# SBUF addresses of attention outputs and of the low part of x's transpose in a two-layer decoder trunk

## The chip, the cores and the metric

The kernel runs on one core of a Trainium2 chip. The metric is the device time of one execution in microseconds; several executions are timed and the median is given. One further execution was profiled.

## What is computed

Two decoder layers on 256 tokens of width 1024, float32 throughout. Cut to what matters:

```python
def hybrid_mixer(x, w_in, w_branch_sb, w_branch_moba, w_out):
    proj = x @ w_in                       # 1024 -> 3*512 + 3*512 + 2*1024
    q_sb, k_sb, v_sb, q_mb, k_mb, v_mb, g_sb, g_mb = jnp.split(proj, cuts, axis=-1)
    o_sb = stick_breaking_attention(heads(q_sb, 8), heads(k_sb, 8), heads(v_sb, 8))
    o_mb = moba_attention(partial_rope(...), partial_rope(...), heads(v_mb, 8))
    merged = jax.nn.sigmoid(g_sb) * (merge_heads(o_sb) @ w_branch_sb) \
           + jax.nn.sigmoid(g_mb) * (merge_heads(o_mb) @ w_branch_moba)
    return merged @ w_out

def swiglu(x, w_gate, w_up, w_down):      # 1024 -> 2816 -> 1024
    return (jax.nn.silu(x @ w_gate) * (x @ w_up)) @ w_down

for l in range(2):
    x = layer_norm(DEEPNORM_ALPHA * x + hybrid_mixer(x, ...), ln_mix_g[l], ln_mix_b[l])
    x = layer_norm(DEEPNORM_ALPHA * x + swiglu(x, ...), ln_ffn_g[l], ln_ffn_b[l])
```

## The kernel before, in words

Each float32 operand of a matmul is split into two parts, hi (rounded to the type float32r) and lo (the rest), and each product is three matmuls: hi by hi, and hi by lo both ways (`mm3`, line 281; every matmul is issued by `mm`, line 275). A matmul has a stationary operand, which a weight load (LDWEIGHTS, engine PEld) puts into the array, and a moving operand, which then streams through it. Every matmul has its own load, and the load of the next runs beside the matmul at work.

The weights stream in as 245 granules of 128 x 1024 from DRAM (`raw`), are cast by ACT (line 48) to `whi`, and subtracted by DVE (line 53) to `wlo`. Ten split granules and four raw ones have fixed places in SBUF. A small planner (`Weave`) decides while the program is built when the side lines (attention, norms, splits) are emitted between the main line of projections; each engine then works in that fixed order.

The stages of a layer, by the names of their PSUM tiles:

- `pvq`, `pk`, `pu`, `pft`: token-major products of x (`tok_major`, line 305). Stationary is a 128-token part of `xT_hi` or `xT_lo`, the weights stream, 512 columns.
- `pqk` (q and k of the sticks), `pg` (gates), `pf` (18 chunks of the gate and up products of SwiGLU): feature-major products of x (`feat_major`, line 327). Stationary are the weights, and `xT_hi` or `xT_lo` streams, 256 columns. The three come in the order (xT_hi, whi), (xT_lo, whi), (xT_hi, wlo).
- `sb_s`, `sb_o` and the like: the attention itself, its results written to `osb_hi/lo` (line 615) and `omb_hi/lo` (line 654).
- `pb`: the branch projections (lines 671 to 685). Stationary are the weights, the attention outputs stream, 256 columns.
- `pw`: the output projection, `pd` and (for the second half of the tokens in the last layer) `pe`: the down projection (`token_out`, line 336). Stationary is the merged branch m or the SwiGLU product h, the weights stream; `pe` in columns of 512, 256 and 256.

All long-lived activations (v, q, k, osb, omb, gates, m, h, layer norm parameters) are 4 KB tiles from one pool `acts` with 15 buffers (line 186), handed out in turn as they become free; x's transpose lies in two tiles of a pool `const` (lines 218 and 219). A tile's address in its partition follows from the pools in the order in which they are made and from the sizes in them. As the built programs place them, in bytes modulo 512:

| tile | before | after |
|---|---|---|
| xT_hi | 384 | 384 |
| xT_lo | 384 | 0 |
| whi, wlo, raw | 448 | 448 |
| osb, omb; h0 and h1 in the same buffers | 448 | 0 |
| v, q_mb, k_mb, gates, m, other h, ln | 448 | 448 |
| work tiles (q, k, attention weights) | 448 | 64 |

Each tile's slices (256 tokens, 128 tokens, 128 weight columns of 4 bytes) begin at multiples of 512 bytes from its start, so that all of them share the tile's place modulo 512.

Of the kernel before, what the change touches and what calls it, by code (L numbers as in the profile page):

```python
# [7 lines left out]
F32 = mybir.dt.float32  # L8
F32R = mybir.dt.float32r
# [5 lines left out]
P = 128  # L15
# [19 lines left out]
class Weave:  # L35
    """Program order: the main line of projections, with side lines (attention, norms,
    rotary, weight splits) woven in. Every engine takes its instructions in program order,
    so each is emitted about when its operands are there, by an estimate of the time at
    which each engine gets through what it has been given. A side line yields the time
    at which it goes on; on the tensor engine's clock."""  # L40

# [40 lines left out]
    def start(self, gen):  # L82
        """A side line whose first stage comes now."""
        side = self.add(gen)
        if not self.busy:
            self._step(side)
        return side
# [9 lines left out]
class WeightStream:  # L97
    """Weight granules [128, 1024]: loaded in float32, then split exactly into
    two float32r parts (hi = rounded, lo = the rest) for the tensor engine."""

# [24 lines left out]
    def line(self):  # L125
        """The side line: a granule at a time, as far as the buffers allow."""
        nc, weave = self.nc, self.weave
        while self.split < self.total:
            g = self.split
            ahead = g - self.current  # L130
            if g > self.limit:
                yield weave.t + 0.1
                continue
            if ahead >= LEAD and max(weave.dve_t, weave.act_t) > weave.t + BACKLOG:
                yield weave.t + 0.2
                continue
            self.load(g + NRAW)
            if ahead > 0:
                yield self.there[g]
            hi, lo = (self.pool.tile([P, GCOLS], F32R, tag=n, name=f"{n}{g}", bufs=NSPLIT)  # L140
                      for n in ("whi", "wlo"))
            t = self.raw.pop(g)
            n = GCOLS // len(self._pieces(g))
            for sl in self._pieces(g):
                e = weave.act(self.there[g], n, nc.scalar.copy, hi[:, sl], t[:, sl])
            if g - self.current > 0:
                yield e
            for sl in self._pieces(g):
                e = weave.dve(e, n, nc.vector.tensor_sub, lo[:, sl], t[:, sl], hi[:, sl].bitcast(F32))
            self.parts[g], self.ready[g] = (hi, lo), e  # L150
            self.split += 1
            self.load(g + 1 + NRAW)

    def allow(self, g):
        """Granule g's buffers are free from here on."""
        self.limit = max(self.limit, min(g, self.total - 1))
# [7 lines left out]


NRAW = 4
NSPLIT = 10
# [12 lines left out]
def hybrid_trunk_kernel(ctx: ExitStack, tc: tile.TileContext, w, xT_in, x_in, ln_in,  # L180
# [4 lines left out]
    wpool = ctx.enter_context(tc.tile_pool(name="wpool", bufs=1))  # L185
    acts = ctx.enter_context(tc.tile_pool(name="acts", bufs=15))
    work = ctx.enter_context(tc.tile_pool(name="work", bufs=3))
# [5 lines left out]

    def unit(name, shape, dt=F32):
        return acts.tile(shape, dt, tag="u4", name=name)

    def pair_tiles(name, shape):
        return unit(name + "_hi", shape, F32R), unit(name + "_lo", shape, F32R)

# [12 lines left out]

# [1 line left out]
    xT_raw = [unit(f"xT_raw{t}", [P, KC, P]) for t in range(2)]  # L214
    ident = const.tile([P, P], F32, name="ident")
    rope = const.tile([P, 2, 2, ROPE], F32, name="rope")
    xs = [const.tile([P, D], F32, name=f"x{t}") for t in range(2)]
    xT_hi = const.tile([P, KC, S], F32R, name="xT_hi")
    xT_lo = const.tile([P, KC, S], F32R, name="xT_lo")
    mask = const.tile([P, 2, P], F32, name="mask")  # L220
    zero = const.tile([P, 1], F32, name="zero")
# [5 lines left out]
    nc.scalar.activation(warm, zero, AF.Sigmoid)  # L227
    # The tensor engine's clock rises after some microseconds of work: give it zeros meanwhile.
    idle = unit("idle", [P, 512], F32R)
# [42 lines left out]

# [1 line left out]
    def mm(o, a, b, start, stop):  # L274
# [30 lines left out]
    def tok_major(o, g, t, first, last, k0):  # L305
        """o[tokens of t, 512] += x @ granule g ([2 kc, 512])."""
        hi, lo = ws.take(g)
        hi = hi.rearrange("p (k c) -> p k c", k=2)
        lo = lo.rearrange("p (k c) -> p k c", k=2)
        for k in range(2):  # L310
            ts = slice(t * P, (t + 1) * P)
            mm3(o, xT_hi[:, k0 + k, ts], xT_lo[:, k0 + k, ts], hi[:, k, :], lo[:, k, :],
                first and k == 0, last and k == 1)

    def both_tokens(name, g0, put):
        """All tokens of x @ granules g0..g0+3; put(tokens, bank) takes each half."""
        acc = [bankM(f"{name}{t}", [P, WIDTH]) for t in range(2)]
        order = ((0, 0), (1, 0), (0, 1), (1, 1), (0, 2), (0, 3)) if g0 == 0 else \
            ((0, 0), (0, 1), (0, 2), (1, 0), (1, 1), (0, 3))
        for t, k in order + ((1, 2), (1, 3)):  # L320
            tok_major(acc[t], g0 + k, t, k == 0, k == 3, 2 * k)
            if t == 1:
                ws.allow(g0 + k + NSPLIT)
            if k == 3:
                put(t, acc[t])

    def feat_major(o, g):
        """o[128 columns, 256 tokens] = (x @ granule g)^T, g [8 kc, 128 columns]."""
        hi, lo = ws.take(g)
# [6 lines left out]
    def token_out(o, g, t, s_hi, s_lo, first, last):  # L336
        """o[tokens of t, 1024] += s^T @ granule g ([1 kc, 1024]); o: (first column, bank) ..."""
        hi, lo = ws.take(g)
# [6 lines left out]

    # Per head, q is stacked as [hi; lo] over the 128 rows and each part of k is there twice,
    # so that q k^T = q_stack (k_hi twice) + q_stack (k_lo twice).
    def stack_q(qs, src, n, c, e):
        """qs[head] [128, ...] from src [2 heads x 64, ...]; the second head is [lo; hi]."""
        for h, (a, b) in enumerate(ROWS):  # L350
# [20 lines left out]
    def rope_line(name, ps, t, put):  # L371
        """Token-major q or k (8 heads x 64) -> rotary -> transposed, handed to put."""
        tmp = work.tile([P, 8, DH], F32, tag="T", name=f"{name}_tok{t}")
# [22 lines left out]
    def scores(s, q, kh, kl, m):  # L396
        """Scores of both heads of a pair: columns 0:128 = (q0, k0), 128:384 = (q1, k0 k1),
        with the causal mask m added to the diagonal blocks."""
        for h in range(2):
# [12 lines left out]
    def weighted(name, p, wt, v, oT, e):  # L412
        """oT[:, p] = (wt @ v)^T for both heads of pair p."""
        yield e + MARGIN
# [93 lines left out]
    def scale_shift(e, x, cols, sub, op, scale, g, b, e_scale):  # L508
        """x <- ((x op sub) g) scale + b; yields each piece of columns as it is done."""
        for c in cols:  # L510
# [7 lines left out]
    def norm_line(name, t, junk, gb):  # L518
        """x_t <- LN(alpha x_t + ps) g + b, and its transpose into xT (split)."""
        x = xs[t]  # L520
# [26 lines left out]
    def last_norm(name, t, banks, gb, down):  # L547
        """The output's tokens: LN(alpha x_t + sum) g + b, blocks of columns in turn."""
        x = xs[t]
# [24 lines left out]

# [1 line left out]
    norms = []  # L576
    for l in range(DEPTH):
        G = l * NG_LAYER
        L = f"l{l}"

        # v of stick-breaking and q of MoBA: tokens 0..127 first
        v_sb = pair_tiles(L + "vsb", [P, 2, WIDTH])
# [28 lines left out]

        # Each pair of stick-breaking heads starts with its q and k; k and v of MoBA and the
        # first gates come between, MoBA's heads after the last sigmoid of stick-breaking, and
        # the gates' sigmoids after the last exponential of MoBA.
        o_sb = pair_tiles(L + "osb", [P, NPAIR, S])
        sides, sigmoids, exps, gates, waiting = [], [], [], [], []

# [35 lines left out]
        weave.finish(ropes)  # L653
        o_mb = pair_tiles(L + "omb", [P, NPAIR, S])
        for p in range(NPAIR):
# [7 lines left out]

        # branch projections and the gated merge, feature-major
        gb = load_gb(l, 0)
# [20 lines left out]

        # output projection: tokens 0..127 first
        norms = []
# [7 lines left out]

        # SwiGLU, first chunks token-major (tokens 0..127 first)
        h_t = [pair_tiles(f"{L}h{i}", [P, 4, S]) for i in range((NFC + 3) // 4)]

# [46 lines left out]

        # down projection: the last granules' tokens 0..127 first
        gb = load_gb(l, 1)
# [108 lines left out]
```

## Time and profile before

| | |
|---|---|
| timed runs | 749.83, 750.5, 754.09 us |
| median | 750.5 us |
| span of the profiled execution (first to last instruction) | 747.6 us |
| median of the timed runs less that span | 2.9 us |
| PE busy | 735.1 us, 98% |
| DVE, ACT, POOL busy | 529.9, 421.8, 13.4 us |
| granted TensorE clock, mean | 0.999 |

The time of the profiled execution by itself, outside the profiler, is not among the runs; its span stands 2.9 us under their median, and the text takes those 2.9 us to lie around the span. PE's busy time is a union of overlapping records: a single matmul's record (some 0.28 us) is longer than the time from its start to the next one's, so the mean duration of one is not its price. The price of one in a row of matmuls that never wait is the length of a piece of the chain of waits divided by its count.

### The profile page before, as it was taken

To read this page: it belongs to the slowest core of one execution; us is meant where nothing else is said; L and a number is where in the kernel's file an instruction comes from. 1 tells how busy PE (TensorE), PEld (TensorE's weight loads), DVE (VectorE), ACT (ScalarE), POOL (GpSimd) and SP (SyncE) were. 2 spreads that over 40 slices of the span, in tenths; PEclk is the share of its full clock that TensorE was granted. 3 is DMA by queue.
4 is the path that set the end of the run, shared out by engine and by line. 5 is a ranking of instruction groups with operands and counts; after the bars stand their busy time and mean duration, and the time that the engine had idled before them with its cause. 6 is when DMAs were issued, how large, how long until landed. Compare 5 with 4: busy or idle time off the path is not lost.

```text
span 747.6 us, 12689 instructions
## 1 busy us (share of the span) xinstructions
PE 735.1 (98%) x5049; PEld 675.5 (90%) x5049; DVE 529.9 (71%) x772; ACT 421.8 (56%) x655; POOL 13.4 (2%) x20
## 2 busy tenths in 40 slices
PE   8999999999999999999999999999999999999996
PEld 5888999998799999988888889999987999999885
DVE  6897878696886666644488878886768866665416
ACT  6788867744565445433267877777435654554300
POOL 0000000000000000000000000000010000000001
PEclk9999999999999999999999999999999999999999
DMA  8864724554586565676168445345635865657501
GB/s 292 284 217 151 221 93 153 176 199 167 178 265 227 181 194 182 198 241 194 60 196 258 146 162 177 108 145 198 210 113 183 277 201 194 196 185 246 166 1 56
DMA packets 39082, 136.31 MB, mean 182 GB/s; under 512 B 4464, under 2 KB 6000, under 8 KB 39024
## 3 DMA queue, kind: packets, MB, share of 16 engines
q1 hardware_dynamic: 39024, 135.51, 55.6%
q8 instruction: 39, 0.64, 0.3%
q14 instruction: 19, 0.16, 0.1%
HBM read 134.45 MB, written 1.05 MB: 181 GB/s over the span
## 4 chain that ended last, share of the span: by engine, by line
PE 84%; DVE 6%; ACT 3%; DMA 3%; issue 2%; POOL 1%; SPq 0%; POOLq 0%; DVEq 0%; ACTq 0%
PE l0pf L275 14%; PE l1pf L275 13%; PE l0pd L275 8%; PE l1pg L275 6%; PE l0pg L275 6%; PE l1pe L275 4%; PE l1pd L275 4%; PE l1pb L275 3%; PE l0pb L275 3%; PE l1pvq L275 3%; DMA raw<-in_w_dram 3%; PE l1pw L275 2%; PE l0pw L275 2%; PE l1pqk L275 2%; DVE wlo L53 2%
## 5 line engine op out<-in xcount | busy, mean ns | idle before, releaser
L53 DVE TENSOR_TENSOR wlo<-raw,whi 128x1024 fp32r<-128x1024 f32 (+1 forms) x245 | 296.8, 1219 | 93.0 <-ACT whi L48 89.5
L48 ACT CAST whi<-raw 128x1024 fp32r<-128x1024 f32 (+1 forms) x245 | 254.1, 1046 | 86.7 <-PE l0pd L275 22.6
L275 PE MATMUL l0pf<-xT_hi,whi 128*128 128x256 f32 x288 | 81.0, 281 | 0.0
L275 PE MATMUL l0pf<-xT_lo,whi 128*128 128x256 f32 x288 | 80.9, 281 | 0.0
L275 PE MATMUL l0pf<-xT_hi,wlo 128*128 128x256 f32 x288 | 80.9, 281 | 0.0
L275 PE MATMUL l1pf<-xT_hi,whi 128*128 128x256 f32 x288 | 79.6, 276 | 0.0
L275 PE MATMUL l1pf<-xT_lo,whi 128*128 128x256 f32 x288 | 79.5, 276 | 0.0
L275 PE MATMUL l1pf<-xT_hi,wlo 128*128 128x256 f32 x288 | 79.5, 276 | 0.0
L275 PEld LDWEIGHTS l0pf<-xT_hi,wlo 128*128 128x128 f32 x288 | 55.3, 192 | 0.0
L275 PEld LDWEIGHTS l0pf<-xT_lo,whi 128*128 128x128 f32 x288 | 54.1, 188 | 0.0
L275 PEld LDWEIGHTS l1pf<-xT_lo,whi 128*128 128x128 f32 x288 | 54.1, 188 | 0.0
L275 PEld LDWEIGHTS l0pf<-xT_hi,whi 128*128 128x128 f32 x288 | 54.1, 188 | 0.0
L275 PEld LDWEIGHTS l1pf<-xT_hi,whi 128*128 128x128 f32 x288 | 54.1, 188 | 0.0
L275 PEld LDWEIGHTS l1pf<-xT_hi,wlo 128*128 128x128 f32 x288 | 54.1, 188 | 0.0
L275 PE MATMUL l0pg<-xT_hi,whi 128*128 128x256 f32 x128 | 35.9, 281 | 0.0
L275 PE MATMUL l1pg<-xT_hi,whi 128*128 128x256 f32 x128 | 35.9, 281 | 0.0
L275 PE MATMUL l0pg<-xT_lo,whi 128*128 128x256 f32 x128 | 35.5, 277 | 0.0
L275 PE MATMUL l1pg<-xT_lo,whi 128*128 128x256 f32 x128 | 35.5, 277 | 0.0
L275 PE MATMUL l1pg<-xT_hi,wlo 128*128 128x256 f32 x128 | 35.4, 277 | 0.0
L275 PE MATMUL l0pg<-xT_hi,wlo 128*128 128x256 f32 x128 | 35.4, 277 | 0.0
L275 PE MATMUL l0pd<-whi,l0h_hi 128*128 128x512 f32 x88 | 34.4, 391 | 0.0
L275 PE MATMUL l0pd<-whi,l0h_lo 128*128 128x512 f32 x88 | 34.3, 389 | 0.0
(379 smaller groups left out, 1821.1 us busy)
## 6 DMA issues: line engine op xcount, KB each, us to landing
raw<-in_w_dram SPq DMA_DIRECT2D x243, 512.0 KB, 4.1
ln<-in_ln_dram SPq DMA_DIRECT2D x8, 512.0 KB, 7.3
xT_raw<-in_xT_dram SPq DMA_DIRECT2D x8, 128.0 KB, 5.0
x<-in_x_dram SPq DMA_DIRECT2D x2, 512.0 KB, 6.4
out_dram<-x SPq DMA_DIRECT2D x3, 256.0 KB, 2.1
raw<-in_w_dram SPq DMA_DIRECT2D x2, 256.0 KB, 3.7
out_dram<-x SPq DMA_DIRECT2D x2, 128.0 KB, 2.0
mask<-in_mask_dram SPq DMA_DIRECT2D x1, 128.0 KB, 3.2
```

What stands on the lines that cost most here:

```text
L48: f(*args, **kw)
L53: f(*args, **kw)
L275: nc.tensor.matmul(o, a, b, start=start, stop=stop)
```

## The change

Two pools are added: `acts2`, with four of the 15 buffers of `acts`, from which osb and omb and later h0 and h1 of the layer are taken, and two one-tile pools of 16 floats (64 bytes) before and behind it. Inside `const` a tile of 128 bytes is put between `xT_hi` and `xT_lo`, and one of 384 bytes behind `xT_lo`. The spacers are written once by POOL and never read. Comments and docstrings are gone as well, which moves line numbers (`mm`, line 275 before, is line 290 after).

```diff
+HALF_LINE = 16
+X_SHIFT = 32
+X_BACK = 96
...
-    acts = ctx.enter_context(tc.tile_pool(name="acts", bufs=15))
+    acts = ctx.enter_context(tc.tile_pool(name="acts", bufs=11))
+    step = ctx.enter_context(tc.tile_pool(name="step", bufs=1))
+    acts2 = ctx.enter_context(tc.tile_pool(name="acts2", bufs=4))
+    step2 = ctx.enter_context(tc.tile_pool(name="step2", bufs=1))
...
-    def unit(name, shape, dt=F32):
-        return acts.tile(shape, dt, tag="u4", name=name)
...
+    for pool_ in (step, step2):
+        nc.gpsimd.memset(pool_.tile([P, HALF_LINE], F32, name="fill"), 0.0)
...
+    def unit(name, shape, dt=F32, home=None):
+        return (home or acts).tile(shape, dt, tag="u4", name=name)
...
     xT_hi = const.tile([P, KC, S], F32R, name="xT_hi")
+
+    nc.gpsimd.memset(const.tile([P, X_SHIFT], F32, name="shift"), 0.0)
     xT_lo = const.tile([P, KC, S], F32R, name="xT_lo")
+    nc.gpsimd.memset(const.tile([P, X_BACK], F32, name="back"), 0.0)
...
-        o_sb = pair_tiles(L + "osb", [P, NPAIR, S])
+        o_sb = pair_tiles(L + "osb", [P, NPAIR, S], acts2)
...
-        o_mb = pair_tiles(L + "omb", [P, NPAIR, S])
+        o_mb = pair_tiles(L + "omb", [P, NPAIR, S], acts2)
...
-        h_t = [pair_tiles(f"{L}h{i}", [P, 4, S]) for i in range((NFC + 3) // 4)]
+        h_t = [pair_tiles(f"{L}h{i}", [P, 4, S], acts2 if i < 2 else None) for i in range((NFC + 3) // 4)]
```

PE, DVE, ACT and SP have the same instructions in the same order in both. Only POOL's row differs; its start before:

```order
L843 MEMSET const-float32-1.0 128x1
L843 MEMSET const-bfloat16-1.0 128x1
L843 MEMSET const-uint8-127 128x1
L853 UNCONDITIONAL_BRANCH
L58 ISA
```

and after, where fill, shift and back are the spacers:

```order
L858 MEMSET const-float32-1.0 128x1
L858 MEMSET const-bfloat16-1.0 128x1
L858 MEMSET const-uint8-127 128x1
L868 UNCONDITIONAL_BRANCH
L204 MEMSET fill 128x16 x2
L232 MEMSET shift 128x32
L234 MEMSET back 128x96
L58 ISA
```

Four memsets have come in ahead of POOL's first work. One wait is of another length: the buffer of `gate1` of each layer is another one, whose former tenant is v's low part, so ACT's copy into it waits for the last group of `sb_o` matmuls. On ACT the whi cast of the next granule stands behind that copy.

## Rows read from the trace of the kernel before

**Rows 1.** The page: busy time, share and count of each engine, and the granted TensorE clock in 40 slices of the span (9 is 90% or more).

```profile
span 747.6 us, 12689 instructions
...
PE 735.1 (98%) x5049; PEld 675.5 (90%) x5049; DVE 529.9 (71%) x772; ACT 421.8 (56%) x655; POOL 13.4 (2%) x20
...
PEclk9999999999999999999999999999999999999999
```

**Rows 2.** The chain of waits that ended last, some of its longest pieces in order of time: start us, length us, engine, tile, line, count of instructions in the piece.

```profile
77.56 5.44 PE l0pg L275 x48
83.92 5.65 PE l0pqk L275 x48
...
99.30 2.83 PE l0pg L275 x24
...
143.10 23.02 PE l0pb L275 x192
...
198.69 4.82 PE l0pft L275 x21
203.73 5.52 PE l0pft L275 x24
...
212.91 2.07 PE l0pf L275 x18
215.20 99.64 PE l0pf L275 x846
314.84 55.08 PE l0pd L275 x243
...
452.02 5.65 PE l1pqk L275 x48
...
467.40 2.83 PE l1pg L275 x24
...
511.20 23.02 PE l1pb L275 x192
...
583.38 95.90 PE l1pf L275 x846
...
718.19 10.91 PE l1pd L275 x48
729.10 11.20 PE l1pe L275 x72
```

**Rows 3.** Busy time by stretches: l0pf, then l1pf. Columns: the stretch, its us; PE, PEld, DVE, ACT and POOL busy with the count of instructions; granted clock; DMA share; GB/s.

```profile
212.75:314.70 101.95, 101.95 (x868) 101.95 (x867) 68.47 (x93) 51.82 (x74) 0.00 (x0) 1.00 0.62 204
580.88:679.10 98.22, 98.22 (x867) 98.22 (x866) 68.29 (x93) 51.84 (x74) 0.00 (x0) 1.00 0.65 211
```

**Rows 4.** The tiles l0pf and l1pf, the weight load that belongs to the matmul (xT_hi, wlo): count, duration in ns (smallest, median, largest), first and last start in us, shape.

```profile
L275 PEld LDWEIGHTS l0pf<-xT_hi,wlo x288: 187/192/192, 212.9 to 314.4; 128*128 128x128 f32 x144
```
```profile
L275 PEld LDWEIGHTS l1pf<-xT_hi,wlo x288: 187/188/192, 581.0 to 678.9; 128*128 128x128 f32 x144
```

**Rows 5.** The tile l0pb, its weight loads by operands (columns as in rows 4).

```profile
L275 PEld LDWEIGHTS l0pb<-l0osb_hi,whi x32: 188/192/192, 142.8 to 164.0; 128*128 128x128 f32 x32
...
L275 PEld LDWEIGHTS l0pb<-l0osb_lo,whi x32: 187/192/192, 142.9 to 164.2; 128*128 128x128 f32 x32
...
L275 PEld LDWEIGHTS l0pb<-l0osb_hi,wlo x32: 187/192/192, 143.1 to 164.3; 128*128 128x128 f32 x32
```

**Rows 6.** POOL's timeline from 0 to 14 us: start us, length us, instruction.

```profile
0.30 0.10 POOL L843 MEMSET const-bfloat16-1.0<- 128x1 bf16 x1
0.33 0.10 POOL L843 MEMSET const-uint8-127<- 128x1 uint8 x1
```

**Rows 7.** Around ACT's copy of gate 1: the last matmuls of the sticks that read v's low part (columns as in rows 4), and ACT's timeline (start us, length us, instruction), in layer 0 and then in layer 1.

```profile
L275 PE MATMUL l0sb_o<-l0sb_ph,l0vsb_lo x8: 282/339/395, 52.6 to 107.1; 128*128 128x512 f32 x4, 128*128 128x256 f32 x4
L275 PE MATMUL l0sb_o<-l0sb_pl,l0vsb_hi x8: 283/338/393, 52.9 to 107.2; 128*128 128x512 f32 x4, 128*128 128x256 f32 x4
```
```profile
107.70 0.21 ACT L48 ACTIVATION_READ_ACCUMULATOR l0mb_e<-l0mb_s,l0mb_nmax 128x1 f32 x1
107.79 0.60 ACT L48 COPY l0gate<-l0pg 128x512 f32<-128x512 f32 x1
108.26 1.08 ACT L48 CAST whi<-raw 128x1024 fp32r<-128x1024 f32 x1
```
```profile
L275 PE MATMUL l1sb_o<-l1sb_pl,l1vsb_hi x8: 283/338/393, 421.3 to 475.3; 128*128 128x512 f32 x4, 128*128 128x256 f32 x4
```
```profile
475.80 0.21 ACT L48 ACTIVATION_READ_ACCUMULATOR l1mb_e<-l1mb_s,l1mb_nmax 128x1 f32 x1
475.89 0.60 ACT L48 COPY l1gate<-l1pg 128x512 f32<-128x512 f32 x1
```

More of the change, by code (lines that the diff above doesn't have):

```diff
@@ L192, in hybrid_trunk_kernel, with pair_tiles @@
     ctx.enter_context(tc.manual_schedule())
-    def unit(name, shape, dt=F32):
-        return acts.tile(shape, dt, tag="u4", name=name)
-    def pair_tiles(name, shape):
-        return unit(name + "_hi", shape, F32R), unit(name + "_lo", shape, F32R)
+    for pool_ in (step, step2):
+        nc.gpsimd.memset(pool_.tile([P, HALF_LINE], F32, name="fill"), 0.0)
+    def unit(name, shape, dt=F32, home=None):
+        return (home or acts).tile(shape, dt, tag="u4", name=name)
+    def pair_tiles(name, shape, home=None):
+        return tuple(unit(f"{name}_{n}", shape, F32R, home) for n in ("hi", "lo"))
     def bankM(name, shape):
```

## The prediction

> **What bounds the kernel now.** I read the page's busy table first: TensorE (PE) is at work for 735.1 of 747.6 us, and its granted clock stands at the upper level, 2.4 GHz, in all 40 slices [rows 1]. So there is neither idle time to win nor a clock to raise; what is left is the pace at which PE goes from one matmul to the next. For that I read the chain of waits, where a piece gives its length and how many matmuls it holds [rows 2]; the quotient is the pace. For one and the same shape, 128x128 by 256 columns, three paces stand there: 95.90 us / 846 = 113.36 ns in l1pf, 99.64 / 846 = 117.78 ns in l0pf, 23.02 / 192 = 119.90 ns in l0pb and l1pb. The 512-column matmuls have two: 55.08 / 243 = 226.67 ns where the SwiGLU product h is the stationary operand (l0pd), 5.52 / 24 = 230 and 4.82 / 21 = 229.5 ns where x's transpose is (l0pft).
>
> Next I asked what else differs between l0pf and l1pf. The table by stretches [rows 3] shows the same DVE work (68.47 and 68.29 us), the same ACT work (51.82 and 51.84), a like DMA share (0.62 and 0.65), clock 1.00 in both, and still 101.95 against 98.22 us for 867 or 868 matmuls. The granules come fast enough for the better pace, since l1pf has it. The tiles' own rows [rows 4] show one more thing: in l0pf the weight load before (xT_hi, wlo), the one that runs while xT_lo streams, has a median of 192 ns; in l1pf 188; in pb, where attention outputs stream, all three loads stand at 192 [rows 5]. A weight load and the streaming operand of the matmul before it seem to disturb each other, more or less by where both lie: by the layout table, pb has both at 448 modulo 512 and pays always, x's transpose is at 384 beside weights at 448 and pays in some stretches only.
>
> **The change part by part.** Instructions first. PE, DVE, ACT and SP get the same instructions in the same order. POOL gets four memsets at its start (to 96 floats wide); its own there take 0.10 us each [rows 6] and its next work is far later, so 0.4 us beside the first loads: 0. One wait is later: the ACT copy of gate 1 now goes into a buffer that v_lo held, so it needs the last sb_o matmul. That starts at 107.2 us at the latest, and the copy starts at 107.79, behind ACT's own exponentials; in layer 1 475.3 against 475.89 [rows 7]. With one matmul of up to 0.39 us after that start some 0.2 us remain. Behind the copy ACT has the whi cast of 108.26 and attention casts; if the cover were gone, the cast would slip by tenths of a us, which PE sees only if its granule is then late. Cost 0, bound +0.5.
>
> The rest is addresses. I cost every group of matmuls whose operands move, by the nearest pace in the trace.
>
> (a) pf, gates and q/k: 1728 + 768 + 384 = 2880 matmuls of 256 columns with x's transpose streaming; one in three streams xT_lo, which moves from 384 to 0 modulo 512. The two paces of these matmuls are 113.36 and 117.78. If the move takes away the disturbed one, l0pf gives back 864 x 4.42 ns = 3.8 us; of the pieces of q/k and gates in [rows 2], the 5.65 of 48 and the 2.83 of 24 lie 0.21 and 0.11 us over 113.36 ns each, in both layers: 0.6 us. l1pf has nothing to give. If it spreads the disturbed pace to all: l1pf +3.8, and of the 1152 gate and q/k matmuls the 1008 outside those four pieces, +4.4. So (a) is between -4.4 and +8.2 us. I take -4.4: the disturbance is seen on the load beside xT_lo alone, and that is the operand that moves.
>
> (b) pb: 2 x 192 matmuls with attention outputs streaming, from 448 to 0. At 113.36 they give 384 x 6.54 = -2.5 us, at 117.78 -0.8; at worst 0, as 119.90 is the slowest pace in these pieces. I take -2.5.
>
> (c) h0 and h1 take the attention outputs' places. They are stationary operands: l0pd 8 chunks x 2 halves x 2 token blocks x 3 = 96, l1pd 48 and l1pe 24 matmuls of 512 columns, 168 in all. Weights at 448 streaming with a stationary operand elsewhere is what l0pft has (229.5): 168 x 2.8 = +0.5 us. Bounds: 0, and the 119.90 pace doubled, 168 x 13.1 = +2.2. Another 48 of l1pe have 256 columns: the 72 of its last piece, less 24 at 227.3 (l1pd, 10.91 / 48), leave 5.74 us, 119.7 ns each; at 113.36 -0.3, at worst 0.
>
> (d) Token-major projections: their third matmul has xT_lo as stationary operand. pvq, pk, pu and pft of both layers are 576 matmuls at about 229.5. Back to 226.67 is -1.6 us; all at twice 117.78 is +3.5. I take 0: the weights that stream there stay at 448, and two of three stationary operands stay at 384.
>
> (e) The work tiles (q, k and the attention weights of the sticks) go from 448 to 64. The matmuls that read them are among the 416 that the page's 5049 [rows 1] leave beside the groups above, the output products and the 7 idle ones. At 6.54 ns each, the widest gap in (a) and (b), that is 2.7 us to either side at most; most of them stand in chains where PE waits for DVE or ACT. I take 0.
>
> Sum: -3.8 - 0.6 - 2.5 + 0.5 - 0.3 = -6.7 us, that is a span of 740.9. The profiled execution's own time is the median of the three before, 750.5, within what its span leaves: 2.9 us lie around it. So 743.8 us. The three runs lie between 749.83 and 754.09, as far apart as one pf stage at the other pace (3.8 us), so the pace of such a stage may well differ from run to run; that weakens what one profile says of l0pf.
>
> The Trainium skill, "TensorE: Matmul & The Clock Gate", in Part 2 under "Step-by-step: what each phase is for", says that PE reads streaming operand and weights through two independent ports and that loading the next weights takes no bandwidth from the running matmul. By that rule addresses could not matter, (a) to (e) would all be 0 and the time 750.5: the first rival below. The trace does not fit the rule in full: three paces at one shape and one clock [rows 2], with slower loads in the slower ones [rows 4, 5].
>
> **The rivals.** First, nothing or little: the three paces come from something that no address sets (the gap at which a stage starts, which then lasts), and only pb gains or not even that. For it: the pace of l0pf changes at its 19th matmul, 2.07 us / 18 = 115.0 before and 117.78 after two transposes, at unchanged addresses, and l1pf has the same addresses as l0pf. Against it: pb holds 119.90 in both layers, and never 113. Times: 750.5 with nothing; 748.0 with pb alone. Chances: nothing 0.12, pb alone 0.10.
>
> Second, slower: the shift puts xT_lo where its stream and the wlo load (448) meet at every start rather than at some, and the disturbed pace holds in every stage that streams x. Place: l1pf and the fast gate pieces; price +8.2 by (a), less 2.5 in pb, with +0.5 in (c): 756.7. It decides once l1pf runs at 117.78 too. If the new pace were pb's 119.90, another 2880 x 2.12 = 6.1 us: 762.8. For it: a stage that keeps a good or a bad pace is on an edge, and a step of 128 bytes can go to either side. Against it: 384 beside 448 is one 64-byte step from the case that always pays; 0 is further off.
>
> A third, in between: (a) and (b) come as forecast, and (c) and (d) at their upper ends, 1.7 and 3.5 us above what I took: 749.0. It counts as no change, chance 0.08.
>
> **How the numbers follow.** Measurement tells about 0.5% from no change, that is 746.7 and 754.3. Forecast 0.52 (its own range 740 to 746.7: the low end with (d) at -1.6 and (e) at -2, the high end with pb at 117.78 and a third of (d)'s upper end). The three cases without a measurable change: 0.30. Slower 0.18, a good half of it under 757. The range from 740 to 756 leaves out the worse half of the slower case (0.09) and a tenth of the forecast at its low end (0.05). Predicted 743.8.
>
> **What would show it.** In the changed kernel's chain l0pf's 846 matmuls should take 95.9 us, both pb pieces of 192 21.8, and l0pf's loads before (xT_hi, wlo) stand at 188. l1pd's chunks 0 to 7 should be a little slower than the rest. Wrong if l0pf still shows 117.78 (address of xT_lo indifferent), if l1pf rises to 99.6 (slower rival), if pb stays at 23.0, or if ACT's copy of gate 1 is shown waiting on PE.

## The result and the profile after

The changed kernel takes 758.22 us (median of 6 runs, 757.81 to 759.49), the kernel before 753.08 us in the runs beside them (749.83 to 754.38): ratio 1.0086, 95% interval 1.0063 to 1.0109 (the ratios here and below are those of the record, not the quotients of the two medians). It is slower, by a little under 1%, and outside the range of the prediction.

The page's busy table of the changed kernel, for [rows 1]:

```profile
span 755.7 us, 12693 instructions
...
PE 744.3 (99%) x5049; PEld 682.9 (90%) x5049; DVE 530.3 (70%) x772; ACT 422.2 (56%) x655; POOL 13.8 (2%) x24
...
PEclk9999999999999999999999999999999999999998
```

PE is 9.2 us longer at work for the same 5049 matmuls, at the same clock. It does not wait more: 11.4 us of the span are left beside its work, 12.5 before. The matmuls themselves follow each other more slowly. Where, the chain of waits shows (columns as in [rows 2]):

```profile
78.29 5.65 PE l0pg L290 x48
84.86 5.66 PE l0pqk L290 x48
...
145.23 22.61 PE l0pb L290 x192
...
200.40 4.91 PE l0pft L290 x21
205.53 5.60 PE l0pft L290 x24
...
217.17 99.65 PE l0pf L290 x846
316.81 55.76 PE l0pd L290 x243
...
515.70 22.61 PE l1pb L290 x192
...
587.61 99.65 PE l1pf L290 x846
...
726.27 10.91 PE l1pd L290 x48
737.17 11.20 PE l1pe L290 x72
```

Against [rows 2], l0pf stands where it was, l1pf has gone from 95.90 to 99.65 us, that is from 113.36 to 117.79 ns a matmul, the first l0pg piece from 113.3 to 117.7 ns. pb has fallen, but to 117.8 ns and not to 113.4. l0pd has risen from 226.7 to 229.5 ns, l0pft from 229.5 to 233.8. l1pf by stretch, for [rows 3]:

```profile
585.27:687.20 101.93, 101.93 (x867) 101.93 (x867) 68.02 (x93) 51.83 (x74) 0.00 (x0) 1.00 0.60 202
```

DVE, ACT and the clock as before; only the us differ. The weight load before (xT_hi, wlo), for [rows 4], has a median between the two values of before, and pb's loads, for [rows 5], are at 187 and 188:

```profile
L290 PEld LDWEIGHTS l1pf<-xT_hi,wlo x288: 187/190/192, 585.2 to 686.9; 128*128 128x128 f32 x144
```
```profile
L290 PEld LDWEIGHTS l0pb<-l0osb_hi,whi x32: 187/188/189, 144.9 to 165.8; 128*128 128x128 f32 x32
...
L290 PEld LDWEIGHTS l0pb<-l0osb_lo,whi x32: 187/187/188, 145.1 to 165.9; 128*128 128x128 f32 x32
```

In pb the loads no longer show a disturbance, and the pace is 117.8 all the same. l0pf tells the same: its loads before (xT_hi, wlo) have come down from a median of 192 to 188, which the prediction named as a sign of the better pace, 113.4, and its matmuls still take 117.8 ns (a line of the page; its last figures are busy us, mean ns and idle us):

```profile
L290 PEld LDWEIGHTS l0pf<-xT_hi,wlo 128*128 128x128 f32 x288 | 54.1, 188 | 0.0
```

So a load's length does not give the pace away, as the prediction took it to.

The sum over the matmuls' starts (each to the next, waits left out), stage by stage, from the first profile of before to this one: pf +3.8 (all of it l1pf), gates +2.8, q/k +0.9, pb -0.8, l0pd +0.7, l1pd +0.1, token-major stages other than l0pv and l0pq about +1.1. Together +8.6; the span grew by 8.1.

### The profile page after: what moved, and what is told of

Same layout as the page of the kernel before. It is cut to its first block, busy times and chain, and to the rows that moved or that the text cites. A ratio compares the mean times of both kernels' runs of the same rounds, so it can differ in the third digit from the quotient of the medians.

```text
span 755.7 us, 12693 instructions
## 1 busy us (share of the span) xinstructions
PE 744.3 (99%) x5049; PEld 682.9 (90%) x5049; DVE 530.3 (70%) x772; ACT 422.2 (56%) x655; POOL 13.8 (2%) x24
## 4 chain that ended last, share of the span: by engine, by line
PE 85%; DVE 5%; ACT 4%; DMA 3%; issue 2%; POOL 1%; SPq 0%; POOLq 0%; DVEq 0%; ACTq 0%
PE l0pf L290 13%; PE l1pf L290 13%; PE l0pd L290 8%; PE l0pg L290 6%; PE l1pg L290 6%; PE l1pe L290 4%; PE l1pd L290 4%; PE l1pb L290 3%; PE l0pb L290 3%; PE l1pvq L290 3%; PE l0pw L290 2%; PE l1pw L290 2%; PE l1pqk L290 2%; DMA raw<-in_w_dram 2%; PE l0pqk L290 2%
## 5 line engine op out<-in xcount | busy, mean ns | idle before, releaser
L290 PE MATMUL l1pf<-xT_lo,whi 128*128 128x256 f32 x288 | 81.3, 282 | 0.0
```

Source lines behind the costliest of these rows:

```text
L290: nc.tensor.matmul(o, a, b, start=start, stop=stop)
```

## The experiments

Three theories stood against each other at first. Theory 1: the place of the streaming operand beside that of the weights sets the pace. Theory 2: the distance between hi and lo does. Theory 3: no address matters; how a stretch of matmuls is entered sets it.

**The disputed cost by itself.** A kernel that has only matmuls: its data is loaded from DRAM and copied to an array, then come stretches of 48 matmuls at chosen places of that array, each behind one or two matmuls of 128 columns ("short matmuls").

```diff
+    for a in range(0, 512, 64):
+        for d in range(0, 512, 64):
+            for gap in (1, 2):
+                stretch(f"h{a}l{d}g{gap}q", a, d, 448, 448, gap)
```

> This kernel leaves out the whole computation of the trunk: it copies x to the output and runs 128 stretches of 48 matmuls of 256 columns in the kernel's order of three (hi,whi) (lo,whi) (hi,wlo), with the weights at 448 modulo 512 and the streaming hi and lo parts at each of the 64 pairs of places in steps of 64 bytes, each pair twice (after one and after two 128-column matmuls). No other engine works beside it. Theory 1 (each streaming operand's place relative to the weights sets the pace): a pair's pace is the mean over its two places, hi weighing twice; with both at 448 119.9 ns as in pb, (384, 384) 113.4 or 117.8, (384, 0) 117.8, and some pairs stay at 113.4 in both visits. Theory 2 (the distance between hi and lo decides, whatever the weights' place): the pairs with hi = lo hold 113.4 wherever they lie, all others 117.8. Theory 3 (no address matters, the pace is set by how a stretch is entered): no pattern over places, and the two visits of a pair differ as often as two pairs do.

Measured: places repeat every 256 bytes, in hi and in lo, to 0.1 ns. So 4 x 4 pairs say all. A pair (a, b) is hi at a and lo at b, modulo 256 from here on: 448 of the layout table is 192 there, 384 is 128, and 304 is 48. Mean ns from start to start, from the ninth matmul of a stretch on, after one / after two short matmuls (hi in rows, lo in columns; weights at 192):

| hi \ lo | 0 | 64 | 128 | 192 |
|---|---|---|---|---|
| 0 | 117.8 / 117.8 | 117.8 / 117.8 | 117.8 / 117.8 | 118.8 / 118.7 |
| 64 | 117.0 / 116.9 | 118.6 / 118.7 | 117.8 / 121.4 | 119.5 / 119.8 |
| 128 | 117.8 / 117.8 | 118.6 / 118.8 | 117.8 / 113.3 | 117.8 / 119.3 |
| 192 | 120.0 / 117.8 | 116.6 / 117.6 | 117.8 / 117.8 | 120.0 / 120.0 |

The kernel before has x's transpose at (128, 128): the one pair with 113.3, and with two paces. The changed kernel has it at (128, 0): 117.8, both times. pb went from (192, 192), 120.0, to (0, 0), 117.8, and these are its paces in the two kernels. Matmuls of four of these stretches in the trace (count, duration in ns, smallest/median/largest, first and last start in us):

```profile
L78 PE MATMUL h384l384g1q<-arena x16: 281/281/282, 793.6 to 798.9; 128*128 128x256 f32 x16
```
```profile
L78 PE MATMUL h384l384g2q<-arena x16: 276/276/277, 799.5 to 804.6; 128*128 128x256 f32 x16
```
```profile
L78 PE MATMUL h384l0g2q<-arena x16: 281/282/283, 729.6 to 734.9; 128*128 128x256 f32 x16
```
```profile
L78 PE MATMUL h448l448g2q<-arena x16: 281/283/284, 904.6 to 910.0; 128*128 128x256 f32 x16
```

From the first to the last start of the 16 is 45 matmuls: 5.1 us where the median is 276, 5.3 at 281 and 282, 5.4 at 283, as the means have it. So 276, 281 and 283 in a row's median stand for 113.3, 117.8 and 120.0. Theory 1 holds in that a place beside the weights sets the pace; its rule of a mean over both places does not, since (192, 64) is under both (192, 192) and (64, 64). Theory 2 falls: hi and lo at one place are at 117.8, 118.6 and 120.0 elsewhere. Theory 3 falls as a whole, but keeps the few pairs whose two visits differ by more than 1 ns: (128, 128), (64, 128), (192, 0) and (128, 192). And no DVE or ACT work and no transfer but some 1 GB/s of instruction loading ran beside these matmuls: PE's own two operands are enough for these paces. The Trainium skill says in "SBUF — State Buffer", section "SBUF: two separate sides", that PE never waits on anyone; as far as other engines go the runs agree, since 113.3, 117.8 and 120.0 with no other engine at work are, to 0.1 ns, the paces of the kernel with DVE busy for 70% of the span. What the prediction drew from the rule of the Trainium skill on the two ports, that addresses could not matter, does not hold: the pace of one shape at one clock runs from 113.3 to 121.4 ns by the two addresses and, at a few pairs, by the matmuls in front.

**Half of the change at a time.** x's shift undone:

```diff
-X_SHIFT = 32
-X_BACK = 96
+X_SHIFT = 0
+X_BACK = 128
...
-    nc.gpsimd.memset(const.tile([P, X_SHIFT], F32, name="shift"), 0.0)
```

> The shift of xT_lo is undone (both parts of x's transpose at 384), the attention outputs stay at 0. Theory 1 and 2: the stages that stream x are again at 113.4 or 117.8 ns as in the kernel before (l1pf's 846 at 95.9 us), pb stays at 117.8 (22.6 us each), so 0.8 us under the kernel before where the same stages are slow: 749 to 753. Theory 3: any stage may be at either pace, l1pf at 99.6 as likely as 95.9; pb 22.6.

Measured 749.04 us, ratio to before 0.9957 (0.9935 to 0.9978). Both pf at 95.90, pb at 22.61, and one piece of the gates for comparison, here and then in the kernel before:

```profile
131.57 4.59 PE l0pg L289 x39
...
145.60 22.61 PE l0pb L289 x192
...
217.27 95.90 PE l0pf L289 x846
```
```profile
129.40 4.44 PE l0pg L275 x39
```

The pools without the shift are a small gain. Only 0.8 us of it is pb; l0pf at the better pace (113.4) gives 3.7 us against the first profile of before, and l0pd (+0.7) and the gates (+1.9) take most of that back. The gates came out at 116.4 and 117.0 ns a matmul, against 114.2 before: at this place the pace of a stage is not given by the places of its own operands alone. What else may set it stands under (e) below.

The shift kept, the attention outputs, h0, h1 and the work tiles back at 448:

```diff
-    for pool_ in (step, step2):
-        nc.gpsimd.memset(pool_.tile([P, HALF_LINE], F32, name="fill"), 0.0)
```

> xT_lo at 0 as in the changed kernel, the attention outputs and the work tiles back at 448. Theory 1 and 2: every stage that streams x at 117.8 (both pf 99.65 us), pb back at 23.0: some 759, a little above the changed kernel's 758.2. Theory 3: between 750 and 759.

Measured 758.14 us, ratio 1.0066 (1.0041 to 1.0091); both pf at 99.65, pb at 23.03, gates at 117.9 and 118.0 ns:

```profile
145.93 23.03 PE l0pb L286 x192
...
588.53 99.65 PE l1pf L286 x846
```

The loss is the shift of xT_lo.

Both parts of x's transpose 128 bytes further on:

```diff
+    nc.gpsimd.memset(const.tile([P, X_SHIFT], F32, name="shift"), 0.0)
     xT_hi = const.tile([P, KC, S], F32R, name="xT_hi")
...
-    nc.gpsimd.memset(const.tile([P, X_SHIFT], F32, name="shift"), 0.0)
     xT_lo = const.tile([P, KC, S], F32R, name="xT_lo")
```

> Both parts of x's transpose 128 bytes further on, at 0 modulo 512; the rest as in the changed kernel. Theory 1: hi and lo lie 64 bytes behind the weights modulo 512, as pb's operands now do, and pb has 117.8 there: every stage that streams x at 117.8, 758. Theory 2: hi and lo at one place again, so 113.4 in most stages and both pf possibly at 95.9: 746 to 752. Theory 3: as for the shift alone.

Measured 758.07 us, ratio 1.0063 (1.0039 to 1.0088), both pf at 117.8. Theory 2 falls in the kernel too. One thing does not fit the map: two gate pieces of layer 1 ran at 113.6 at this place, which the map never shows there.

xT_lo shifted by a whole turn of 256 bytes, the rest as in the changed kernel:

```diff
-X_SHIFT = 32
-X_BACK = 96
+X_SHIFT = 64
+X_BACK = 64
```

> xT_lo shifted by 256 bytes instead of 128 (hi at 384, lo at 128 modulo 512), the rest as in the changed kernel. Theory 1: 256 is a whole turn, so the stages that stream x are at 113.4 or 117.8 ns as with no shift, pf at 95.9 in at least one layer, 747 to 754. Theory 2 (any distance between hi and lo costs): both pf 99.65, 758.

Measured 749.37 us, ratio 0.9933 (0.9907 to 0.9958), both pf at 95.90:

```profile
215.93 95.90 PE l0pf L290 x846
...
581.85 95.90 PE l1pf L290 x846
```

Not the distance, but the place modulo 256.

**Finer steps, and the entry.** A second map:

```diff
+    for a in range(256, 512, 16):
+        for gap in (1, 2, 3):
+            stretch(f"fine{a}g{gap}q", a, a, 448, 448, gap)
+    for a in range(256, 512, 64):
+        for b in range(256, 512, 64):
+            for gap in (1, 2, 3):
+                stretch(f"wh{a}wl{b}g{gap}q", 384, 384, a, b, gap)
```

> Leaves out the whole computation, as the first map: only stretches of matmuls, x copied to the output. In the first map no place but (384, 384) beside weights at 448 showed 113.3 ns, and only in the visit after two 128-column matmuls; places repeated every 256 bytes. Asked here: (1) the stretch at (384, 384) after 0 to 7 short matmuls, each twice in a row: theory 1, now with a state that the entry sets and the place keeps, says 113.3 or 117.8 by the number of short matmuls and the same in both repeats; a pace drawn by chance at each entry would differ between repeats. (2) hi and lo together in steps of 16 bytes: theory 1 allows a place with 113.3 after each of three entries; if the pace goes by 64-byte places alone, the four steps inside one show the same. (3) hi and lo of the weights at the 16 pairs of places with x at 384: 113.3 only where both lie at 448 (or 64 bytes after x). (4) 24 matmuls of 512 columns with the parts of x stationary at 16 pairs of places and the weights streaming at 448: the pair (448, 448) at 226.7 ns as in l0pw and l0pd, (384, 384) some 229.5, (384, 256), which is (384, 0) again modulo 256, some 233 as in the changed kernel's l0pft.

Measured: (1) All 16 stretches at (128, 128) were at 113.3, after 0 to 7 short matmuls; 15 of them stand behind a stretch at that pace, the first directly behind one at 119.8. (2) 16-byte steps differ, so 64-byte places are not the unit. hi and lo at 48 modulo 256 showed 113.7 / 113.3 / 113.7 after the three entries, at 128 again 117.8 / 113.3 / 113.3; the other 14 places lay between 116.6 and 120.1.

```profile
L78 PE MATMUL fine304g1q<-arena x16: 275/275/281, 308.9 to 314.1; 128*128 128x256 f32 x16
```

(3) With x at 128, weights hi and lo at (192, 192) gave 113.3 in all three, hi at 192 with lo at 64 113.5 / 113.3 / 113.3, (64, 64) 113.3 in one of three visits, and two more pairs 115.6 or 115.7 in one or two; the expectation had not allowed for 192 with 64. (4) 512 columns, x stationary at (192, 192) 227.3 / 226.7, (128, 128) 228.9, (128, 0) 233.5 / 228.9: the first two near the stages of before (226.7 and 229.5), the third, in one of its two visits, as the changed kernel's l0pft.

A third map puts a stretch at (128, 0) in front, then 0 to 5 short matmuls, then the stretch in question:

```diff
+            stretch(f"pa{r}x{gap}q", 384, 0, 448, 448, 1)
+            stretch(f"sa{r}x{gap}q", 384, 384, 448, 448, gap)
```

> Leaves out the whole computation, as the maps before. (1) A stretch at hi = 384, lo = 0 (always slow in the first map), then 0 to 5 short matmuls of 128 columns, then a stretch at (384, 384), all twice; and the same with a stretch at 48 modulo 256 behind. Theory 1 with a carried state: after 0 or 1 short matmuls (384, 384) goes on at 117.8, after 2 or more some entries give 113.3, the same in both repeats; the place 48 gives 113.3 to 113.7 after every entry. If the pace were drawn at each entry by chance, repeats differ, and the place 48 is no exception. (2) 24 matmuls of 512 columns with both parts of x stationary, in steps of 16 bytes, weights streaming at 448: 448 at 226.7 to 227.3, 384 at 228.9 to 229.5, 304 some 233.3 as in the token-major stages of the kernel with everything at 48.

Measured, in both repeats alike: (128, 128) goes on at 117.8 with no short matmul between, and is at 113.3 with 1 to 5. The place 48 is at 113.5 to 113.8 after each.

```profile
L77 PE MATMUL sa0x0q<-arena x16: 278/281/281, 167.6 to 172.9; 128*128 128x256 f32 x16
```
```profile
L77 PE MATMUL sa0x2q<-arena x16: 276/276/335, 190.6 to 195.8; 128*128 128x256 f32 x16
```

One short matmul was enough here, where the expectation asked for two; in the first two maps, behind other stretches, one was not. So at this place a stretch at 117.8 passes its pace on to the next, and an interruption may change it; a pace of 119.8 from another place was not passed on in the second map. In steps of 16 bytes the stationary operand of 512-column matmuls gave 226.7 at 192, 228.9 at 128, 233.3 at 48.

**The two times of the kernel before.** Its runs fall near 750 or near 755. The same kernel, twice more:

> The kernel before, unchanged, for a second profile: its timed runs fall near 750 or near 755. Theory 1 with a state that the entry sets: near 750 one of the two pf stages is at 113.4 and the other at 117.8 (95.9 and 99.6 us), near 755 both at 117.8; pb 23.0 in both cases. If the two times had another origin (transfers, the clock), pf would read the same as in the first profile.

> The same once more, for the other of the two times if the first look shows the same one as before; same expectations.

Measured 751.12 and 754.58 us. The first has l0pf at 99.64 and l1pf at 95.90 as before, the second:

```profile
144.25 23.02 PE l0pb L275 x192
...
216.34 99.64 PE l0pf L275 x846
...
512.11 23.02 PE l1pb L275 x192
...
584.34 99.64 PE l1pf L275 x846
```

The difference of 3.5 us fits one pf stage at the other pace (3.74).

**Better places.** All streaming operands at 48 modulo 256; xT in its tile and the four outputs in theirs begin 16 bytes in, since tiles come at multiples of 32:

```diff
+    def placed(name):
+        t = const.tile([P, KC * S + 8], F32R, name=name)
+        return t[:, STEP:STEP + KC * S].rearrange("p (k s) -> p k s", k=KC)
...
+    def four(name):
+        t = acts2.tile([P, 16 * S + 8], F32R, tag="u16", name=name)
+        return [t[:, o:o + 4 * S].rearrange("p (k s) -> p k s", k=4) for o in range(4, 16 * S, 4 * S)]
```

> Both parts of x's transpose and the attention outputs at 48 modulo 256, weights at 448 (192 modulo 256): the place where the second map showed 113.3 to 113.7 ns after each of three entries. Theory 1 (the place of the streaming operand beside the weights modulo 256 sets the pace, and at 384 the entry chooses between two): both pf 95.9 to 96.2 us, all gates and q/k pieces at 113.3 to 114, pb some 21.8 each, so against the run with both parts at 384 and outputs at 0 (749.0) 1.7 us less in pb and up to 2.6 in the gates: 743 to 747, with the token-major stages, whose stationary operand then lies at a place not mapped, worth up to 2 us to either side. Theory 4 (the maps hold only where no other engine touches SBUF): no order in the paces, pf between 113.3 and 120.

Measured 747.1 us (746.84 to 747.4), ratio 0.9907 (0.9883 to 0.9932); pf and pb in both layers:

```profile
144.91 21.76 PE l0pb L301 x192
...
204.35 5.60 PE l0pft L301 x24
...
216.01 95.92 PE l0pf L301 x846
...
509.56 21.76 PE l1pb L301 x192
...
580.69 95.94 PE l1pf L301 x846
```

Theory 4, named in the expectation, falls: the map's places hold in the kernel, and in four runs there is no second time. It stands 0.1 us above the expected range: the gates are at 115.0 where 113.3 to 114 was expected, and the token-major stages, with x stationary at 48, pay 233.3 instead of 229.5, 576 x 3.8 = 2.2 us.

Only the attention outputs at 48, x at 384 as before:

> Only the attention outputs (and h0, h1) at 48 modulo 256; x's transpose at 384 as in the kernel before. Theory 1: pb 21.8 each instead of 22.6 at 0 and 23.0 at 448; the stages that stream x as the entry has it: 746 to 751. Theory 4: pb stays at 22.6 or above.

Measured 748.69 to 749.6 in four runs, 752.23 to 753.78 in six (ratio 0.9975, 0.995 to 1.0001); pb 21.83 as expected, and both pf at 99.64 in the profile, which is one of the second kind. Two times again, as the kernel before has them, and the six lie above the expected range.

**A short matmul ahead.** To this, h0 and h1 at 192 and, in front of the second SwiGLU chunk of each layer:

```diff
+            if c == NTOK_FC + 1:
+                short = xT_hi[:, 0, 32:32 + P]
+                for _ in range(2):
+                    nc.tensor.matmul(ps[:, 0, :P], short, short, start=True, stop=True)
```

> x's transpose at 384 as in the kernel before, attention outputs at 48 and h0, h1 at 192 modulo 256 (weights at 192), and in front of the second SwiGLU chunk of each layer two matmuls of 128 columns whose result is overwritten. Theory 1 with an entry that chooses and a pace that is kept: as in the maps the short matmuls bring the place 384 to 113.3, so the 816 matmuls behind them take 92.5 us in both layers in every run instead of 92.5 or 96.1; the times have one value and not two, near 745 (outputs at 48 alone: 749 or 753). If the entry is drawn by chance or set by transfers, the two values stay: 748 and 752.

Measured 744.88 us (744.36 to 745.4), ratio 0.9877 (0.9844 to 0.991). The chain at l0pf, with the short matmuls (line 763) in the middle:

```profile
215.04 3.54 PE l0pf L292 x30
218.58 0.17 PE l0pf L763 x2
218.75 1.30 PE l0pf L292 x11
```
```profile
218.75 92.53 PE l0pf L292 x816
...
578.32 3.54 PE l1pf L292 x30
582.02 92.55 PE l1pf L292 x816
```

118.0 ns ahead of the two, 113.4 behind them, in both layers: the same places, one interruption. With one short matmul instead:

> The same with one short matmul instead of two. By the third map one is enough after a slow stretch, by the first it was not: either the same 745 in every run, or both pf at 117.8 and 752 in every run; two values from run to run would speak for chance.

Measured 745.14 us (744.73 to 745.54), ratio 0.9881 (0.9854 to 0.9909), 92.55 and 92.54 for the 816. One is enough here, and the eight runs of the two kernels have one time.

Everything at 48 and h0, h1 at 192:

> All streaming operands at 48 modulo 256 as in the run before that, and h0, h1 at 192, where 512-column matmuls with both at one place took 226.7 ns: 168 matmuls by some 2.8 ns, 0.5 us less than 747.1, so 746.6; pf and pb unchanged at 95.9 and 21.8. Nothing gained if the pace of l0pd goes by something other than the place of the stationary operand.

Measured 746.25 us (745.52 to 747.01), ratio 0.9896 (0.9868 to 0.9925); l0pd's 243 took 55.12 us against 55.80 at 48. The intervals of the ratios of this run and of that with h0, h1 at 48 overlap, but the stage shows the term.

## Why the prediction was wrong

**The bound.** Right: PE's pace is all that moved, at full clock, and for 256 columns its paces in the two kernels are those named, 113.4, 117.8 and 119.9. For 512 columns one came in that was not named, 233.3.

**(a), the step that failed.** The prediction read 113.36 as the pace of these matmuls and 117.78 as a disturbance that a move would take away, because the load beside xT_lo was longer in l0pf. It is the other way round: of the 16 pairs of places in steps of 64 bytes beside these weights, 15 never reach 113.4, and (128, 128), where before had both parts, is the one that does, at times. Moving xT_lo left the only good pair of that map. Priced at -4.4, measured +7.5 (pf +3.8, gates +2.8, q/k +0.9); the upper bound, +8.2, held. The slower rival was this case, with its place, l1pf and the fast gate pieces, and 756.7 us from it; it was given a chance of 0.18, and the stated range ended at 756, below that rival's own time. Of the 15.3 us between the sum as forecast (-6.7) and as measured (+8.6), (a) is 11.9.

**(b)** Taken -2.5, measured -0.8: the place 0 has 117.8, the second of the two paces named there. **(c)** Taken +0.5 for h0 and h1, measured about +0.8. l0pd's 229.5 is the mean over moved and unmoved chunks: the moved ones stand at 233.3, the others at 226.7 as before, so 0.7 us over 96 matmuls or 7 ns each, not 2.8; the stationary place 0 is at 233.5 in the maps. In l1pd, where every six matmuls alternate with nine of pe, the moved chunks went from 231 to 232 only. The mechanism was right, the size low in one layer and high in the other. The -0.3 for l1pe's 256-column matmuls did not come: pe's pieces of nine in the moved chunks took 1.39 to 1.41 us, 1.39 before. **(d)** Taken 0, measured about +1.1: that two of three stationary operands stay was no reason, since the map has 233.5 for x stationary at (128, 0) in one of its two visits, against 228.9 at (128, 128).

**(e)** Taken 0. In the changed kernel nothing of it can be told, since the run with the shift alone has its gates at 118 with the work tiles back at 448 too. With x at (128, 128) something can. The gates took 116.4 to 117.0 ns in the two profiles with the work tiles at 64 and the attention outputs at 0 (x's shift undone, and a shift of 256 bytes), and 114.1 or 114.2 in all six profiles with the work tiles at 192 modulo 256 (the place 448 of before), among them those with the outputs at 48. That is 1.9 us or more. The work tiles are read by the attention matmuls between the gate pieces, and one of them, SwiGLU's sg, by the two transposes in front of pf's 19th matmul; and the 15 runs of the first two lie together, from 747.75 to 750.24, where the kernel before and that with the outputs at 48 have two times. So the price of a moved tile may lie in the matmuls behind those that read it. No run moved the work tiles alone, so this is not shown.

**The edits costed at nothing.** The memsets start at 0.72 to 0.86 us on POOL, behind its own [rows 6], and take 0.12 to 0.18 us. ACT's copy of gate 1 follows ACT's own work as before, for [rows 7]:

```profile
108.82 0.22 ACT L48 ACTIVATION_READ_ACCUMULATOR l0mb_e<-l0mb_s,l0mb_nmax 128x1 f32 x1
108.91 0.60 ACT L48 COPY l0gate<-l0pg 128x512 f32<-128x512 f32 x1
```

**The base.** 750.5, the median of three runs, was one of two times. The profile taken had l1pf at the better pace, the last of its three profiles, at 754.58 us, had neither stage there, and of the 25 runs beside the first experiments 14 lie above 753. The prediction named the two paces as a likely cause of the spread, and still put one number under the sum. Against an execution with both pf at 117.8 (span 752.3) the changed kernel (755.7) loses 3.4 us of span, not 8.1.

**What stays open.** Why the places matter in this way, why the period is 256 bytes and why 48 and 128 are the good ones beside 192 was not found: the maps are tables, not a mechanism. Why a pf stage of the kernel before enters one pace in one execution and the other in the next was not found either; that an interruption at the entry can change the pace, which is then kept, is shown. Whether the places of the short matmul's own operands matter was not tried, nor was a move of the work tiles alone. The maps' stretches are short, and the run with both parts at 0 has gate pieces at a pace that its map lacks.

## What to carry to other kernels

Where PE is busy all the time at full clock, divide pieces of the chain by their counts, stage by stage: one shape at two paces is worth 4% of it, and here came from the addresses of its two operands. Before moving an operand to cure the worse pace, map the pace over the places with matmuls alone; the better one may be the exception that the present place allows. And where runs of one kernel lie as far apart as the change is worth, take more profiles before the sum is made: here the second showed the same as the first, and the third showed the other time and its stage.

## What the runs showed of the hardware

- The pace of 128x128 by 256 float32r matmuls with a load each ran in the maps from 113.3 to 121.4 ns by the places of weights and streaming operand modulo 256 bytes, at a few places also by the matmuls in front; that of 512 columns from 226.7 to 234.5.
- At one place, (128, 128) beside weights at 192, a pace once taken was kept over 846 matmuls, and one 128-column matmul ahead, of 0.06 us (two took 0.17), changed it from 118.0 to 113.4 ns in both layers: worth up to 3.7 us a stage.
- A weight load of 192 ns instead of 188 went with the pace of 120.0; at 117.8 loads stood at 187 to 192.
